# The first load of a low-rank update kernel as two transfers: 16 partitions, then 112

## The chip, the cores and the metric

The kernel runs on one core of a Trainium2 chip. The metric is device time in microseconds (us) for one execution, the median of the runs shown; lower is better. Engines are named as in the profile: PE (TensorE, matrix multiply), PEld (its weight loads), DVE (VectorE), ACT (ScalarE), POOL (GpSimd) and SP (SyncE, which here issues all DMA transfers; SPq is its queue). The core has 16 DMA engines, which all transfers share.

## What is computed

```python
def setup_inputs():
    batch, seq, d_model, r = 16, 512, 768, 16
    return {
        "x": np.random.randn(batch, seq, d_model).astype(np.float32),
        "A": np.random.randn(d_model, r).astype(np.float32) * 0.1,
        "B": np.random.randn(r, d_model).astype(np.float32) * 0.1,
        "scale": 0.5,
    }

def reference(x, A, B, scale):
    lora = np.matmul(np.matmul(x, A), B)
    return (x + scale * lora).astype(np.float32)
```

x is 8192 rows ("tokens") of 768 float32, 25.2 MB; the result is as large. A and B are 48 KB each.

## The kernel before

**Tiling.** The 8192 tokens lie in five parts of 8, 8, 16, 16 and 16 tokens per partition (`PARTS`). Within a part, partition p holds S consecutive tokens, so that n tokens of a partition are one contiguous run of n x 3072 bytes in memory (`memory`, L96 to L98). `x_all` in SBUF has room for 48 tokens a partition, the first four parts; the last part reuses the room of the first two. The work is done in 8 groups of 8 tokens per partition.

**Loads and stores.** `LOADS` (L106) cuts the parts into eight loads (part, first token, tokens): the first part is loaded as 2 tokens and then 6, the later ones as 8 or 16. Load k counts 16 on its own semaphore `s_load[k]` when it has landed. `STORES` (L129) has five stores. Everything goes through SP's one queue, in the order of `on_sync` (L136): load 0, load 1, a wait for POOL's memset of `a_rows` (`s_ready`), three transfers of A with 4 rows each, a wait for the memset of `b_rows`, the transfer of B with 16 rows (to every fourth partition of the first 64), loads 2 to 5, then stores 0 and 1 once the first two groups are summed, loads 6 and 7 as the room of the first part comes free, and the other stores. The last store stands behind the section, at L356 of the profile's kernel.

**Compute.** For each group: POOL and ACT cast x to float16 (`narrowed`, L188 to L199; it waits for the load that holds the tokens, once for each engine and load), DVE transposes in blocks of 32x32 (L255), PE multiplies with a block diagonal form of A (L285), ACT scales and spreads the product (L240), PE multiplies with B (L306), and DVE adds the result to x in place (L260). For group 0, POOL casts the first two tokens (from load 0), ACT the other six (from load 1). POOL also builds the operands from A and B at the start: `b_half` (L214) waits for B's rows, and DVE's transpose of A's rows (L248) for `s_a`, which counts the three transfers of A and POOL's first cast.

Of the kernel before, what the change touches and what calls it, by code (L numbers as in the profile page):

```python
# [28 lines left out]
def kernel(  # L29
# [10 lines left out]
    P = 128  # L40
# [3 lines left out]
    x2 = x.flatten_outer_dims()  # L44
# [38 lines left out]
    def sem(name):  # L83
        sems.append(nc.alloc_semaphore(name))
        return sems[-1]
# [10 lines left out]
    def memory(t2, i, s, n):  # L96
        S = PARTS[i]
        return t2[ds(parts[i], S * P), :].rearrange("(p s) d -> p s d", s=S)[:, ds(s, n), :]  # L98

    def held(i, s, n):  # L100
        return tiles(where.index((i, s)), n)

    def tiles(t, n):
        return x_all[:, ds(t % ROOM, n), :]

    LOADS = [  # L106
        (0, 0, 2), (0, 2, 6), (1, 0, 8), (2, 0, 8), (2, 8, 8), (3, 0, 16), (4, 0, 8), (4, 8, 8)
    ]
    s_load = [sem(f"s_load{k}") for k in range(len(LOADS))]

    def load_of(t):
        i, s = where[t]
        return next(k for k, ld in enumerate(LOADS) if ld[0] == i and ld[1] <= s < ld[1] + ld[2])
# [21 lines left out]

    def on_sync(e):  # L136
        def load(k):
            ld = LOADS[k]
            e.dma_start(out=held(*ld), in_=memory(x2, *ld)).then_inc(s_load[k], 16)  # L139

        def summed(k):
            e.wait_ge(s_sum, k + 1)
            if STORED[k] + 1 < NG:

                e.sem_inc(s_free[PAIRS - 1], 1)

        def store(k, done):
            st = STORES[k]
            e.dma_start(out=memory(out2, *st), in_=held(*st)).then_inc(done, 16)

        load(0)
        load(1)
        e.wait_ge(s_ready, 1)
        blocks = A.rearrange("(c e) r -> c (e r)", e=64)
        for c in range(SETS):
            e.dma_start(
                out=a_rows[c : SET * SET : SET, :], in_=blocks[ds(c * SET, SET), :]
            ).then_inc(s_a, 16)
        e.wait_ge(s_brows, 1)
        e.dma_start(out=b_rows[0 : R * APART : APART, :], in_=B).then_inc(s_b, 16)  # L160
        for k in range(2, len(LOADS) - 2):
            load(k)

        for p in range(2, PAIRS):
            e.sem_inc(s_free[p], 1)
        summed(0)
        summed(1)


        e.wait_ge(s_lora, 2 * PAIRS + 2)  # L170
        store(0, s_out0)
        store(1, s_out1)
        e.wait_ge(s_out0, 16)
        load(len(LOADS) - 2)
        e.wait_ge(s_out1, 16)
        load(len(LOADS) - 1)
        for k in range(2, len(STORES)):
            summed(k)
            if k == 2:


                e.wait_ge(s_raise, 6)
            if k + 1 < len(STORES):
                store(k, s_out)
# [3 lines left out]
    def narrowed(e, copy, g, first, n=SUB):  # L188
        t = g * GROUP + first
        for k in dict.fromkeys(load_of(t + k) for k in range(n)):  # L190
            if (e, k) not in here:
                here.add((e, k))
                e.wait_ge(s_load[k], 16)
        if g:
            e.wait_ge(s_taken, g)
        ins = copy(out=xn[:, ds(first, n), :], in_=tiles(t, n))  # L196

        ins.then_inc(s_narrow if g else s_first if first else s_a, 1)

    def on_gpsimd(e):  # L200
        e.memset(a_rows[0:Q], 0.0).then_inc(s_ready, 1)  # L201
        e.memset(b_rows, 0.0).then_inc(s_brows, 1)  # L202
        e.memset(pick, 0.0).then_inc(s_pick, 1)
        e.memset(w_bd.rearrange("p c k m -> p (c k m)").bitcast(fp32), 0.0)  # L204
        e.memset(y_bd.rearrange("p s m -> p (s m)").bitcast(fp32), 0.0).then_inc(s_ready, 1)  # L205
        e.wait_ge(s_pick, 1)
        e.affine_select(  # L207
            out=pick, in_=pick, compare_op=mybir.AluOpType.not_equal, fill=1.0, base=0,
            pattern=[[0, NQ], [-APART, Q]], channel_multiplier=1,
        ).then_inc(s_pick, 1)  # L210
        narrowed(e, e.tensor_copy, 0, 0, SUB // 2)
        e.wait_ge(s_pick, 2)
        e.wait_ge(s_b, 16)
        e.tensor_copy(out=b_half, in_=b_rows).then_inc(s_bh, 1)  # L214
        e.wait_ge(s_ready, 3)
        e.tensor_copy(  # L216
            out=w_one.rearrange("i (c e) k r -> i c e (k r)", c=SETS),
            in_=a_t[0:Q].rearrange("i k r (e c) -> i c e (k r)", c=SET)[:, 0:SETS, 0:SET, :],
        ).then_inc(s_w, 1)
        e.wait_ge(s_w, 1)  # L220
        for b in range(NQ):
            e.tensor_copy(  # L222
                out=w_bd[ds(b * Q, Q), :, :, ds(b * Q, R)], in_=w_one
            ).then_inc(s_w, 1)
            e.wait_ge(s_w, b + 2)
        for g in range(1, NG):
            narrowed(e, e.tensor_copy, g, SUB)

    def on_scalar(e):
        narrowed(e, e.copy, 0, SUB // 2, SUB // 2)  # L230
        narrowed(e, e.copy, 0, SUB)
        e.wait_ge(s_bp, 1)
        e.copy(out=b_mm, in_=lora[0][:, 0, :]).then_inc(s_bm, 1)  # L233
        for g in range(NG):
            if g + 1 < NG:
                narrowed(e, e.copy, g + 1, 0)
            e.wait_ge(s_y, g + 1)
            for b in range(NQ):
                q = ds(b * Q, Q)
                last = e.mul(out=y_bd[q, :, q], in_=y_ps[q, :, :], mul=sc)  # L240
                if b == 0 and g + 1 < NG:

                    last.then_inc(s_narrow, 1)
            last.then_inc(s_spread, 1)
# [151 lines left out]
```

## Time and profile before

| | us |
|---|---|
| median of 3 runs | 123.53 (123.52 to 123.67) |
| the profiled execution, its own time | 123.47 |
| its span, first to last instruction | 121.7 |
| granted TensorE clock, mean | 0.913 |

The span is the time between the first and the last profiled instruction of one execution; the rest of its time, 1.8 us, lies around it. The page gives for each engine its busy time and share, and cuts the span into 40 slices:

```profile
DMA  3999999999998997999999999997998899799790
GB/s 65 442 418 440 444 420 428 444 420 428 477 517 355 420 517 307 452 412 436 452 396 428 460 404 436 469 517 323 452 517 388 388 517 436 339 517 452 323 517 0
```

A digit is the mean busy share of the 16 DMA engines in that slice of 3 us, in tenths, and below it is what they moved in GB/s. Other views used are: the stretches (busy time by engine, DMA share and rate in chosen windows), the timeline of one engine, the waits (who waited for whom: total us, times, longest), the chain of waits (the chain that ended last, followed back from the last instruction) and the list of DMA issues with sizes and the time from issue to landing. In the timeline, "x2" is a merged run of two instructions, whose duration includes what lies between them. A DMA-issuing instruction ends when the transfer is handed on, long before its data has landed.

### The profile page before, as it was taken

To read this page: it belongs to the slowest core of one execution; us is meant where nothing else is said; L and a number is where in the kernel's file an instruction comes from. 1 tells how busy PE (TensorE), PEld (TensorE's weight loads), DVE (VectorE), ACT (ScalarE), POOL (GpSimd) and SP (SyncE) were. 2 spreads that over 40 slices of the span, in tenths; PEclk is the share of its full clock that TensorE was granted. 3 is DMA by queue.
4 is the path that set the end of the run, shared out by engine and by line. 5 is a ranking of instruction groups with operands and counts; after the bars stand their busy time and mean duration, and the time that the engine had idled before them with its cause. 6 is when DMAs were issued, how large, how long until landed. Compare 5 with 4: busy or idle time off the path is not lost.

```text
span 121.7 us, 889 instructions
## 1 busy us (share of the span) xinstructions
PE 50.7 (42%) x322; PEld 29.6 (24%) x322; DVE 81.7 (67%) x42; ACT 37.4 (31%) x43; POOL 28.4 (23%) x24
## 2 busy tenths in 40 slices
PE   0000239477457647745745744774674320000000
PEld 0000026243323424423423322442442110000000
DVE  0002850599999999999999989999995991000000
ACT  4003928526409313644440192733004000000000
POOL 7721638017009002604400170710000000000000
PEclk9999999999999999999999999999999995555555
DMA  3999999999998997999999999997998899799790
GB/s 65 442 418 440 444 420 428 444 420 428 477 517 355 420 517 307 452 412 436 452 396 428 460 404 436 469 517 323 452 517 388 388 517 436 339 517 452 323 517 0
DMA packets 1928, 50.43 MB, mean 414 GB/s; under 512 B 236, under 2 KB 236, under 8 KB 392
## 3 DMA queue, kind: packets, MB, share of 16 engines
q1 hardware_dynamic: 1928, 50.43, 97.0%
HBM read 25.26 MB, written 25.17 MB: 414 GB/s over the span
## 4 chain that ended last, share of the span: by engine, by line
DVE 34%; DMA 28%; PE 10%; ACT 9%; issue 1%; SPq 0%; POOLq 0%
DVE x_sb L260 22%; DMA x_sb<-in_x_dram 20%; DVE xt L255 12%; DMA out_dram<-x_sb 8%; PE ps_yt L285 6%; ACT xn L196 6%; PE lora_ps L306 3%; ACT y_bd L240 3%; SPq L139 0%; SPq L391 0%; POOLq L134 0%; POOLq L377 0%
## 5 line engine op out<-in xcount | busy, mean ns | idle before, releaser
L260 DVE TENSOR_TENSOR x_sb<-x_sb,lora_ps 128x1536 f32<-128x1536 f32 x32 | 53.7, 1734 | 1.4 <-PE lora_ps L306 1.4
L306 PE MATMUL lora_ps<-b_mm,y_bd 128*128 128x512 f16 (+1 forms) x128 | 25.0, 328 | 22.4 <-ACT y_bd L240 14.1
L196 ACT CAST xn<-x_sb 128x3072 f16<-128x3072 f32 (+1 forms) x9 | 23.4, 2609 | 35.4 <-DMA x_sb<-in_x_dram 25.7
L285 PE MATMUL ps_yt<-xt,w_bd 128*128 128x256 f16 x192 | 26.1, 288 | 12.7 <-DVE xt L255 12.7
L255 DVE STREAM_TRANSPOSE xt<-xn 128x3072 f32<-128x3072 f32 (+1 forms) x9 | 27.0, 3005 | 6.5 <-ACT y_bd L240 6.1
L196 POOL CAST xn<-x_sb 128x3072 f16<-128x3072 f32 (+1 forms) x8 | 20.7, 2586 | 44.7 <-DMA x_sb<-in_x_dram 26.2
L285 PEld LDWEIGHTS ps_yt<-xt,w_bd 128*128 128x128 f16 x192 | 18.9, 101 | 20.6 <-issue 15.8
L306 PEld LDWEIGHTS lora_ps<-b_mm,y_bd 128*128 128x128 f16 x128 | 10.6, 98 | 35.3 <-ACT y_bd L240 16.4
L240 ACT ACTIVATE y_bd<-ps_yt 32x256 f16<-32x256 f32 x32 | 12.0, 374 | 19.5 <-PE ps_yt L285 19.1
L248 DVE STREAM_TRANSPOSE a_t<-a_rows 32x1024 f32<-32x1024 f32 x1 | 1.9, 1943 | 11.3 <-DMA a_rows<-in_A_dram 11.3
L319 PE MATMUL lora_ps<-b_half,pick 128*128 128x512 f16 (+1 forms) x2 | 0.8, 500 | 12.5 <-POOL b_half L214 12.5
L319 PEld LDWEIGHTS lora_ps<-b_half,pick 128*128 128x128 f16 x2 | 0.1, 106 | 12.5 <-issue 12.5
L222 POOL COPY w_bd<-w_one 32x384 f16<-32x384 f16 x4 | 2.0, 499 | 0.2
L214 POOL CAST b_half<-b_rows 128x768 f16<-128x768 f32 x1 | 0.8, 827 | 4.6 <-DMA b_rows<-in_B_dram 4.6
L196 ACT ACT_TABLE_LOAD x1 | 1.3, 1283 | 0.9 <-PEq L377 0.9
L204 POOL MEMSET w_bd<- 128x1536 f32 x1 | 1.4, 1372 | 0.0
L201 POOL MEMSET a_rows<- 32x1024 f32 x1 | 0.9, 941 | 0.5 <-POOLq L134 0.5
L216 POOL CAST w_one<-a_t 32x384 f16<-32x384 f32 x1 | 0.8, 849 | 0.9 <-DVE a_t L248 0.9
L233 ACT CAST b_mm<-lora_ps 128x768 f16<-128x768 f32 x1 | 0.8, 798 | 0.0
L202 POOL MEMSET b_rows<- 128x768 f32 x1 | 0.7, 727 | 0.0
L205 POOL MEMSET y_bd<- 128x512 f32 x1 | 0.5, 514 | 0.0
L207 POOL TENSOR_SCALAR_AFFINE_SELECT pick<-pick 128x128 f16<-128x128 f16 x1 | 0.3, 298 | 0.0
(5 smaller groups left out, 0.6 us busy)
## 6 DMA issues: line engine op xcount, KB each, us to landing
out_dram<-x_sb SPq DMA_DIRECT2D x3, 6144.0 KB, 19.4
x_sb<-in_x_dram SPq DMA_DIRECT2D x5, 3072.0 KB, 14.6
x_sb<-in_x_dram SPq DMA_DIRECT2D x1, 6144.0 KB, 41.6
out_dram<-x_sb SPq DMA_DIRECT2D x2, 3072.0 KB, 13.8
x_sb<-in_x_dram SPq DMA_DIRECT2D x1, 2304.0 KB, 9.7
x_sb<-in_x_dram SPq DMA_DIRECT2D x1, 768.0 KB, 4.6
a_rows<-in_A_dram SPq DMA_DIRECT2D x3, 16.0 KB
b_rows<-in_B_dram SPq DMA_DIRECT2D x1, 48.0 KB, 7.5
```

Source lines behind the costliest of these rows:

```text
L196: ins = copy(out=xn[:, ds(first, n), :], in_=tiles(t, n))
L201: e.memset(a_rows[0:Q], 0.0).then_inc(s_ready, 1)
L204: e.memset(w_bd.rearrange("p c k m -> p (c k m)").bitcast(fp32), 0.0)
L214: e.tensor_copy(out=b_half, in_=b_rows).then_inc(s_bh, 1)
L222: e.tensor_copy(out=w_bd[ds(b * Q, Q), :, :, ds(b * Q, R)], in_=w_one).then_inc(s_w, 1)
L240: last = e.mul(out=y_bd[q, :, q], in_=y_ps[q, :, :], mul=sc)
L248: e.transpose(out=a_t[0:Q].rearrange("i k r c -> i (k r) c"), in_=a_rows[0:Q].rearrange("c (i k r) -> c (k r) i", k=2, r=R),).then_inc(s_r ...
L255: return e.transpose(out=ts[0], in_=ts[1])
L260: ins = e.tensor_tensor(out=xs, in0=xs, in1=lora[p % 2], op=mybir.AluOpType.add)
L285: mm = e.matmul(y_ps, w_bd[:, c, k, :], xv[:, :, c, :, k], start=(m == 0), stop=(m == MMS - 1),)
L306: mms.append(e.matmul(t[:, k, ds(n0, w)], y_bd[:, 2 * p + k, :], b_mm[:, ds(n0, w)], start=True, stop=True,))
L319: last = e.matmul(lora[0][:, 0, ds(n0, w)], pick.rearrange("p b r -> p (b r)"), b_half[:, ds(n0, w)], start=True, stop=True,)
```

## The change

Load 0, 2 tokens of each of 128 partitions (128 rows of 6144 bytes, 768 KB), is issued as two transfers on the same queue, one after the other: partitions 0 to 15, then partitions 16 to 127. Both count on `s_load[0]`, so whoever waits for load 0 waits for 32 counts and not 16 (`needs`). All other loads stay single transfers of 128 partitions, in the same order.

```diff
+    HEAD = 16
+    SHARES = {0: [(slice(0, HEAD), slice(0, 2)), (slice(HEAD, P), slice(0, 2))]}
+    needs = [16 * len(SHARES.get(k, [0])) for k in range(len(LOADS))]
...
         def load(k):
-            ld = LOADS[k]
-            e.dma_start(out=held(*ld), in_=memory(x2, *ld)).then_inc(s_load[k], 16)
+            i, s, n = LOADS[k]
+            for rows, cols in SHARES.get(k, [(slice(0, P), slice(s, s + n))]):
+                n = cols.stop - cols.start
+                e.dma_start(
+                    out=held(i, cols.start, n)[rows], in_=memory(x2, i, cols.start, n)[rows]
+                ).then_inc(s_load[k], 16)
...
             if (e, k) not in here:
                 here.add((e, k))
-                e.wait_ge(s_load[k], 16)
+                e.wait_ge(s_load[k], needs[k])
```

## The prediction

> **What bounds the kernel now.** I read the page's DMA lines first, because the page gives no compute engine more than 67% of the span.
>
> ```profile
> span 121.7 us, 889 instructions
> PE 50.7 (42%) x322; PEld 29.6 (24%) x322; DVE 81.7 (67%) x42; ACT 37.4 (31%) x43; POOL 28.4 (23%) x24
> q1 hardware_dynamic: 1928, 50.43, 97.0%
> DMA packets 1928, 50.43 MB, mean 414 GB/s; under 512 B 236, under 2 KB 236, under 8 KB 392
> ```
>
> One queue carries 50.43 MB, and its packets occupy 97.0% of the time of 16 DMA engines over the whole span. To see where the other 3% lie I cut the span into stretches (columns: stretch, length, busy time of five engines with instruction counts, granted clock, DMA share, GB/s).
>
> ```profile
> 0.00:0.90 0.90, 0.00 (x0) 0.00 (x0) 0.00 (x0) 0.01 (x1) 0.20 (x4) 1.00 0.00 0
> 0.90:1.90 1.00, 0.00 (x0) 0.00 (x0) 0.00 (x0) 1.00 (x1) 0.93 (x2) 1.00 0.00 0
> 1.90:2.90 1.00, 0.00 (x0) 0.00 (x0) 0.00 (x0) 0.27 (x1) 1.00 (x4) 1.00 1.00 147
> 2.90:4.40 1.50, 0.00 (x0) 0.00 (x0) 0.00 (x0) 0.00 (x0) 1.50 (x2) 1.00 0.97 385
> ...
> 5.10:9.90 4.80, 0.00 (x0) 0.00 (x0) 0.00 (x0) 0.00 (x0) 1.46 (x1) 1.00 1.01 434
> 9.90:11.10 1.20, 0.00 (x0) 0.00 (x0) 0.00 (x0) 0.02 (x1) 0.00 (x0) 1.00 1.12 466
> 11.10:44.70 33.60, 19.32 (x114) 11.24 (x114) 27.33 (x14) 17.65 (x18) 11.91 (x9) 1.00 1.00 432
> 44.70:55.00 10.30, 5.95 (x40) 3.55 (x40) 10.30 (x6) 4.25 (x5) 2.75 (x1) 1.00 1.00 432
> 55.00:74.40 19.40, 10.84 (x75) 6.68 (x76) 19.03 (x11) 8.50 (x10) 5.49 (x2) 1.00 1.01 433
> 74.40:101.50 27.10, 14.61 (x95) 8.13 (x93) 25.06 (x14) 5.75 (x9) 2.75 (x1) 0.98 1.00 433
> 101.50:119.40 17.90, 0.00 (x0) 0.00 (x0) 0.00 (x0) 0.00 (x0) 0.00 (x0) 0.50 0.99 428
> ```
>
> From 5.1 us to 119.4 us the queue never starves: 428 to 466 GB/s in every stretch, through all waits of the compute engines. So the time is the moment at which the stream reaches full rate, plus the bytes at about 433 GB/s, plus the tail. The change can act only on the start. There, nothing moves before 1.90, and the first microsecond carries 147 GB/s although the engines count as fully occupied: the first rows are in flight, but come slowly. Measured against 434 GB/s, the ramp has lost (434-147)x1.0/434 = 0.66 us by 2.90 and (434-385)x1.5/434 = 0.17 us more by 4.40: 0.83 us in all.
>
> Next the transfers of SyncE (SPq), which issues all of them, in order of time (start us, duration us). The first two were also looked at singly, and stand first.
>
> ```profile
> 0.89 0.38 SPq L139 DMA_DIRECT2D x_sb<-in_x_dram  x1
> 1.33 0.41 SPq L139 DMA_DIRECT2D x_sb<-in_x_dram  x1
> ```
>
> ```profile
> 1.94 2.00 SPq L156 DMA_DIRECT2D a_rows<-in_A_dram  x3
> 3.98 0.54 SPq L160 DMA_DIRECT2D b_rows<-in_B_dram  x1
> 4.57 2.04 SPq L139 DMA_DIRECT2D x_sb<-in_x_dram  x4
> 44.70 0.82 SPq L149 DMA_DIRECT2D out_dram<-x_sb  x2
> 55.01 7.84 SPq L139 DMA_DIRECT2D x_sb<-in_x_dram  x2
> ```
>
> The first load is issued at 0.89 and its first bytes move at 1.90, 1.01 us later. The second issue starts 0.44 us after the first (1.33-0.89).
>
> Last, what waits for the start, and how much margin it has:
>
> ```profile
> POOL b_half L214 <- DMA b_rows<-in_B_dram: 4.6, 1, 4.6
> POOL xn L196 <- DMA x_sb<-in_x_dram: 0.7, 1, 0.7
> ```
>
> ```profile
> 1.33 9.72 DMA x_sb<-in_x_dram
> 44.70 10.29 DMA out_dram<-x_sb
> ```
>
> ```profile
> x_sb<-in_x_dram SPq DMA_DIRECT2D x1, 6144.0 KB, 41.6
> x_sb<-in_x_dram SPq DMA_DIRECT2D x1, 2304.0 KB, 9.7
> x_sb<-in_x_dram SPq DMA_DIRECT2D x1, 768.0 KB, 4.6
> ```
>
> The 768 KB load lands 4.6 us after its issue, at about 5.5, and GpSimd's cast waits 0.7 us for it; after it GpSimd idles another 4.6 us for B's rows. The chain of waits does not even pass through the first load: it goes from SyncE's second issue through the 9.72 us of the second load. The 6144 KB load, last of the four issued from 4.57 on (issue near 6.2), lands near 6.2+41.6 = 47.8, while the first stores are issued at 44.70: compute is 3.1 us early for the queue.
>
> **The change, part by part.** All against the profiled execution: span 121.7 us, its own time 123.47 us, against 123.53 us, the median of the runs; I carry the difference to the median, so +0.06 goes to every time below.
>
> *Bytes.* The same 768 KB in 128 rows of 6 KB. The head is 16 rows, 96 KB (98,304 bytes); the rest is 112 rows, 672 KB. Sixteen engines have 1 and 7 rows each where they had 8. Sixteen more semaphore writes, one an engine, ride on the queue: 0 to 0.01 us, since the 236 packets under 512 bytes that the queue carries already, the semaphore writes among them, leave it at 433 GB/s.
>
> *SyncE.* One more issue, 0.38 to 0.41 us long and 0.44 us from start to start. The rest's issue starts at 1.33 instead of being part of the one at 0.89, the second load's at about 1.77 instead of 1.33, and it ends near 2.19. The transfers of A would start then and not at 1.94: +0.25 us for A, B and the four loads behind them, because SyncE stood from 1.74 to 1.94 for GpSimd's memset (0.97 to 1.91) anyway. Each is covered by the queue: the second load is needed only when the first is through, about 4.5 us; A and B pass when the second load is through, near 9.9; the loads issued at 4.57 are needed at 10.5. Covers of 2 to 5 us, against 0.25 to 0.44 us; without them each would cost its own delay on the stream. I take nothing for them.
>
> ```profile
> 0.97 0.94 POOL L201 MEMSET a_rows<- 32x1024 f32 x1 [0.53 <-POOLq L134]
> ```
>
> *The wait.* GpSimd's first cast now needs 32 semaphore counts. If the load lands some tenths later, so does the cast; behind it on GpSimd stands only the wait for B's rows with its 4.6 us, which hides it. ScalarE waits for the second load, which moves with the stream. The margin of 3.1 us at the first stores moves with the stream on both sides and stays. Nothing else is late next.
>
> *The start of the stream* is the only term. Seven rows an engine now come with an issue that starts 0.44 us later. In that time each engine has one row: 98,304 bytes at 434 GB/s is 0.23 us of work. With equal latency for both transfers the stream falls behind by 0.44-0.23 = **+0.21 us**. The trace shows no transfer cut this way, so I bound the term from both sides.
> - Below: if the rest finds the path warm, its bytes flow from 1.33+1.01 = 2.34 at full rate, 672 KB/434 GB/s = 1.59 us, and are through at 3.93. Now they are through at 4.54 (147+578 = 725 KB by 4.40, the other 62 KB at 434 GB/s in 0.14). That is -0.61 us, the floor.
> - Above: the head gives no cover at all (+0.44), and its rows are slow besides: 98 KB at the ramp's 147 GB/s take 0.67 us instead of 0.23, another 0.44. Together +0.88 us.
>
> The nearest row to a cut transfer in a filled queue is the stretch 9.9 to 11.1, where A's and B's transfers of 4 and 16 rows pass at 466 GB/s without loss; the nearest row to rows that start cold is 147 GB/s. The head starts cold, so I add a third of its 0.44, 0.15 us, to the 0.21: **+0.36 us**, from which 123.47+0.36+0.06 = 123.89 us.
>
> A page speaks against the change here. The Trainium skill, "SBUF — State Buffer", section "Door 1: The DMA port swizzle", says that the sixteen partitions 0 to 15 reach only 4 of 16 ports, some 109 GB/s. By it the head's 96 KB would take 0.90 us, the term would be about 0.21+0.67 = +0.88, and the time 124.4 (an estimate from that page). No run here shows it yet: B's sixteen rows, passing at 466 GB/s, go to partitions four apart.
>
> **The rivals.**
>
> *The head is spread badly (slower still).* The sixteen rows go to sixteen neighbouring partitions, and 112 rows are dealt out otherwise than 128; if engines get in one another's way, or the head isn't one row an engine at all, the whole of the upper price of slow rows counts: 0.21+0.44 = +0.65, 124.18 us. For it: 147 GB/s with all engines occupied shows that an occupied engine can move little. Against it: 466 GB/s with B's rows among the traffic.
>
> *It is hidden (same).* At 147 GB/s sixteen rows take 0.67 us, more than the 0.44 us until the rest arrives, so the queue may never run dry, and the rest meets engines still busy with the head: 0, 123.53 us. Against it: those eight rows are in flight together now, and reads asked for 0.44 us later can't come back as early.
>
> *The head warms the path (faster).* The slow part is the first row of an engine, not the number of rows; a head of sixteen starts all engines at once and pays the 0.66 us of the first microsecond while the rest is being issued. It gains as soon as the rest's own ramp costs less than the 0.61 us by which it could be early; with half of it paid, -0.30 us, 123.23 us. For it: the ramp is as large as 0.83 us, and of its first 1.0 us only a third is bytes. Against it: bytes can't move before 1.01 us after an issue, and the rest's issue is 0.44 us later. The Trainium skill ("Perfetto Trace Analysis", section "DMA Optimizations") says that splitting transfers can let some start sooner if the DMA engines are generally idle; here they are idle only before 1.90, which is where this rival would have to find its gain.
>
> **How the numbers follow.** The forecast, slower by arrival, has 0.42, with its own range 123.70 to 124.10; the bad spread 0.14; hidden 0.15; faster 0.29. No change means within 0.2%, 0.25 us, about what a measurement of this kernel can tell. Of the forecast 0.04 falls under that, of the faster case 0.02. Slower: 0.38+0.14 = 0.52; same: 0.15+0.04+0.02 = 0.21; faster: 0.27. The range runs from the faster case, 123.2, to the upper bound, 123.53+0.88 = 124.4.
>
> **What would show it.** SyncE: issues of the first load at 0.89 and near 1.33, the second load's near 1.77, A's near 2.2. Stream: the stretch 1.9 to 2.9 under 147 GB/s if the forecast holds, clearly over it in the faster case; the sum of bytes moved by 5 us decides between all four. From 5 us on every stretch again at 428 to 434 GB/s, only shifted, and the last landing, now 101.5+19.4 = 120.9, shifted by the same.
>
> ```profile
> L356 SPq DMA_DIRECT2D out_dram<-x_sb x1: 333/333/333, 101.5 to 101.5; - x1
> DMA to landing us min/median/max: 19.4/19.4/19.4
> ```
>
> I am wrong if the stream reaches 434 GB/s earlier than now, if the tail moves by another amount than the start, or if a stretch after 5 us loses rate.

## The result, and the profile after

The changed kernel takes 124.44 us (median of 4 runs, 124.38 to 124.85), the kernel before beside it 123.58 us (123.52 to 123.67). The ratio is 1.0076, 95% interval 1.0053 to 1.0099: slower by 0.94 us (0.65 to 1.22). The forecast was slower, 123.89 us, with a range up to 124.4; the direction held, and the loss is over twice the forecast one and just outside the range.

The stretches of the changed kernel, in the columns used before:

```profile
0.90:1.90 1.00, 0.00 (x0) 0.00 (x0) 0.00 (x0) 1.00 (x1) 0.93 (x2) 1.00 0.00 0
1.90:2.90 1.00, 0.00 (x0) 0.00 (x0) 0.00 (x0) 0.27 (x1) 1.00 (x4) 1.00 1.12 184
2.90:4.40 1.50, 0.00 (x0) 0.00 (x0) 0.00 (x0) 0.00 (x0) 1.50 (x2) 1.00 0.81 279
4.40:5.10 0.70, 0.00 (x0) 0.00 (x0) 0.00 (x0) 0.00 (x0) 0.42 (x2) 1.00 1.31 342
5.10:9.90 4.80, 0.00 (x0) 0.00 (x0) 0.00 (x0) 0.00 (x0) 1.47 (x1) 1.00 1.02 411
9.90:11.10 1.20, 0.00 (x0) 0.00 (x0) 0.00 (x0) 0.00 (x0) 0.00 (x0) 1.00 0.82 341
11.10:44.70 33.60, 18.47 (x111) 10.98 (x112) 26.57 (x14) 17.68 (x18) 11.92 (x9) 1.00 1.04 444
44.70:55.00 10.30, 6.33 (x45) 3.77 (x43) 10.30 (x6) 4.25 (x5) 2.75 (x1) 1.00 0.92 394
55.00:74.40 19.40, 10.78 (x75) 6.40 (x72) 18.18 (x10) 7.11 (x7) 5.50 (x2) 1.00 1.01 431
74.40:101.50 27.10, 15.02 (x96) 8.41 (x96) 25.43 (x14) 7.14 (x13) 2.75 (x1) 1.00 1.03 442
```

Nothing moves before 1.90, as before. The first stretch, with the head's sixteen rows and the first of the rest, has 184 GB/s instead of 147: a little quicker, not slower. Then the stream stays behind: 279 where it had 385, 342 where it had 456 (the row of the kernel before stands below), still 411 where it had 434, and 341 where it had 466. A row of data counts in the stretch in which it starts, so short stretches are rough: the 341 stands for rows that started just outside, and the 394 further down comes to 432, as before, together with the 444 ahead of it. If each row's bytes are counted evenly over its time in the trace, the changed stream is behind by 0.44 us at 5 us, 0.86 at 8, 0.86 at 11 and 0.99 at 20 (bytes short, at 434 GB/s).

```profile
4.40:5.10 0.70, 0.00 (x0) 0.00 (x0) 0.00 (x0) 0.00 (x0) 0.42 (x2) 1.00 1.16 456
```

The same in the list of issues (KB each, median us from issue to landing) and in the chain of waits (start us, us):

```profile
x_sb<-in_x_dram SPq DMA_DIRECT2D x1, 672.0 KB, 5.1
x_sb<-in_x_dram SPq DMA_DIRECT2D x1, 96.0 KB, 2.4
```

```profile
0.89 0.39 SPq L146
1.28 0.06 issue
1.35 0.40 SPq L146
1.75 0.04 issue
1.79 10.13 DMA x_sb<-in_x_dram
```

The rest is issued at 1.35 and lands 5.1 us later, at 6.45; the uncut load landed at 5.49. The second load is issued at 1.79 and lands at 11.92, before at 1.33+9.72 = 11.05. So 0.87 us are lost by the time the second load has landed, as much as the medians differ by (124.44-123.58 = 0.86). The profiled execution itself took 124.85 us, the most of the four and 1.38 more than the profiled one before; its other 0.5 us came later. By the even count the stream is 1.01 us behind at 70 us and 1.28 at 118. What happens after 70 us was not followed; the other three runs, 124.38 to 124.47, have no profile, but are too short for all of it.

### The profile page after: what moved, and what is told of

Same layout as the page of the kernel before. It is cut to its first block, busy times and chain, and to the rows that moved or that the text cites. A ratio compares the mean times of both kernels' runs of the same rounds, so it can differ in the third digit from the quotient of the medians.

```text
span 123.1 us, 890 instructions
## 1 busy us (share of the span) xinstructions
PE 50.6 (41%) x322; PEld 29.6 (24%) x322; DVE 81.7 (66%) x42; ACT 37.5 (30%) x43; POOL 28.4 (23%) x24
## 4 chain that ended last, share of the span: by engine, by line
DVE 34%; DMA 29%; PE 10%; ACT 9%; issue 1%; SPq 1%; POOLq 0%
DVE x_sb L269 22%; DMA x_sb<-in_x_dram 21%; DVE xt L264 12%; DMA out_dram<-x_sb 9%; PE ps_yt L294 6%; ACT xn L205 6%; PE lora_ps L315 3%; ACT y_bd L249 3%; SPq L146 1%; SPq L400 0%; POOLq L139 0%; POOLq L386 0%
## 6 DMA issues: line engine op xcount, KB each, us to landing
x_sb<-in_x_dram SPq DMA_DIRECT2D x1, 6144.0 KB, 42.4
```

## The experiments

Three theories. A, arrival: after the head the engines have too little to do until the second issue. B, span: a transfer into only some of the partitions makes engines write the same neighbourhood of SBUF, and the 112 rows pay for that. C: the sixteen rows of the head, all in one neighbourhood, are slow. A was the forecast's main term, C stood behind the 0.15 us added to it, and B was part of a rival. Losses below are (ratio-1) times the median of the kernel before in the same runs, with the interval's ends. The ratio is not that of the two medians; in the row of even and odd rows these differ by 1.77.

| kernel | us | before | ratio (95%) | loss, us |
|---|---|---|---|---|
| changed | 124.44 | 123.58 | 1.0076 (1.0053 to 1.0099) | 0.94 (0.65 to 1.22) |
| changed, again | 124.63 | 123.52 | 1.0095 (1.0074 to 1.0117) | 1.17 (0.91 to 1.45) |
| small columns first | 123.74 | 123.32 | 1.0043 (1.0030 to 1.0056) | 0.53 (0.37 to 0.69) |
| large columns first | 123.57 | 123.52 | 1.0013 (0.9999 to 1.0028) | 0.16 (-0.01 to 0.35) |
| 112 rows, then 16 | 124.61 | 123.32 | 1.0111 (1.0096 to 1.0126) | 1.37 (1.18 to 1.55) |
| head extra, 128 rows uncut | 123.96 | 123.32 | 1.0058 (1.0044 to 1.0071) | 0.72 (0.54 to 0.88) |
| 112 rows alone | 123.91 | 123.41 | 1.0041 (1.0026 to 1.0055) | 0.51 (0.32 to 0.68) |
| 64 rows, then 64 | 125.25 | 123.32 | 1.0155 (1.0141 to 1.0170) | 1.91 (1.74 to 2.10) |
| 64 and 64, read apart | 125.11 | 123.52 | 1.0141 (1.0125 to 1.0157) | 1.74 (1.54 to 1.94) |
| even rows, then odd | 125.29 | 123.52 | 1.0119 (1.0084 to 1.0153) | 1.47 (1.04 to 1.89) |
| two queues | 124.61 | 123.41 | 1.0082 (1.0055 to 1.0109) | 1.01 (0.68 to 1.35) |

**Columns in place of partitions, small piece first.**

```diff
+    CUTS = {0: [(0, 192), (192, 2 * D)]}
+    needs = [16 * len(CUTS.get(k, [0])) for k in range(len(LOADS))]
...
+            for c0, c1 in CUTS.get(k, []):
+                o, m = (v.rearrange("p s d -> p (s d)")[:, c0:c1] for v in (held(*ld), memory(x2, *ld)))
+                e.dma_start(out=o, in_=m).then_inc(s_load[k], 16)
```

> Load 0 is cut by columns and not by partitions: first 192 of the 1536 numbers of all 128 partitions (the same 96 KB, 768-byte rows), then the other 1344. Issues and bytes are those of the changed kernel, but every transfer has 128 partitions. Theory A (arrival: too little work is queued until the second issue) expects the changed kernel's loss here too, 0.2 us or more over the kernel before, up to the whole 0.86. Theory B (the 112 rows, dealt seven to an engine, make engines write the same partitions' neighbourhood) and theory C (the sixteen neighbouring rows of the head are slow) expect 0 to +0.2 us.

It lost 0.53 us, so a loss is there without any transfer that spans fewer than 128 partitions; but it is about half of the changed kernel's. Its stretches show where:

```profile
1.90:2.90 1.00, 0.00 (x0) 0.00 (x0) 0.00 (x0) 0.27 (x1) 1.00 (x4) 1.00 0.69 147
2.90:4.40 1.50, 0.00 (x0) 0.00 (x0) 0.00 (x0) 0.00 (x0) 1.50 (x2) 1.00 0.82 294
4.40:5.10 0.70, 0.00 (x0) 0.00 (x0) 0.00 (x0) 0.00 (x0) 0.42 (x2) 1.00 1.31 472
5.10:9.90 4.80, 0.00 (x0) 0.00 (x0) 0.00 (x0) 0.00 (x0) 1.46 (x1) 1.00 1.03 433
```

The loss is in 2.9 to 4.4: the DMA engines are occupied for 0.82 of the time, where the uncut load had 0.97, and move 294 GB/s for 385. From 4.4 on the rate is full. (The 0.69 in the first microsecond is no sign of the gap: the next kernel, without a gap, has 0.67 there.) The changed kernel is not yet at its full rate there (342 and 411), so something else goes on in it.

**The same cut, large piece first.**

```diff
-    CUTS = {0: [(0, 192), (192, 2 * D)]}
+    CUTS = {0: [(0, 1344), (1344, 2 * D)]}
```

> The cut by columns with the large piece (1344 of 1536 columns) first. Same two transfers as in the cut with the small piece first, other order. If the +0.42 us there came from arrival (A: too little is queued until the second issue), it is gone: 0 +-0.15 us. If a transfer more costs in itself, or rows of 768 bytes do, it stays: +0.3 to +0.5 us.

0.16 us, with an interval that touches 0. The same two sizes, in the order in which the queue does not run short, cost under a third of it, and in the stretch in which the other order lost, the rate is nearly that of the uncut load:

```profile
2.90:4.40 1.50, 0.00 (x0) 0.00 (x0) 0.00 (x0) 0.00 (x0) 1.50 (x2) 1.00 0.95 367
```

So a second transfer and rows of 768 bytes are not it, and the 0.53 us are mostly A.

**The 112 rows first, the 16 behind them.**

```diff
-    SHARES = {0: [(slice(0, HEAD), slice(0, 2)), (slice(HEAD, P), slice(0, 2))]}
+    SHARES = {0: [(slice(HEAD, P), slice(0, 2)), (slice(0, HEAD), slice(0, 2))]}
```

> The same two transfers, the 112 partitions first and the 16 behind them. Eight engines' rows are never short of work while the second issue is made, so A expects 0 (within 0.2 us of the kernel before). B expects +0.6 us or more, with long packets while the 112 rows move. C expects +0.4 us or more, with the loss only at the end of the load, when the sixteen rows move.

Here 112 rows are queued ahead of the second issue, the engines are occupied from 1.9 to 4.4 (0.94 and 1.03), and yet the loss is larger, 1.37 us. A alone falls with this run: with the first piece large enough, what is left is the span of the transfers, of the 112 rows or of the sixteen.

**The head as an extra, with load 0 uncut.**

```diff
+    spare = sb("spare", [16, 2, D], fp32)
...
+        e.dma_start(out=spare, in_=memory(x2, 0, 0, 2)[0:16]).then_inc(s_load[0], 16)
         load(0)
...
-                e.wait_ge(s_load[k], 16)
+                e.wait_ge(s_load[k], 32 if k == 0 else 16)
```

> The sixteen-row transfer goes first, into a spare buffer of 16 partitions, and load 0 follows uncut with its 128 partitions; 96 KB more are moved and nothing is computed from them. It has the head and no transfer of 112. The uncut load starts one issue later, so A expects +0.44 us (0.23 of extra bytes and the 0.21 of the gap). B expects no more than that, +0.2 to +0.44. C expects the head's own slowness on top, +0.8 us or more, with long packets in the head or right behind it.

0.72 us, of which 0.23 are the extra 96 KB; the other 0.49 (0.31 to 0.65) agree with the 0.53 (0.37 to 0.69) of the cut by columns, where the first piece lay over all partitions. So sixteen neighbouring rows at the cold start cost nothing that shows beside the gap behind them; intervals this wide leave room for a tenth or two. The trace of the changed kernel agrees: the head's rows take 360 ns each on average and are through at 2.46, when the first rows of the rest, from 2.38 on, have only begun. C falls for this place, as far as these runs can tell. Behind a full queue, as in the run above, they are not so cheap, or the 112 rows cost more without the gap; the two were not told apart.

**The 112 rows alone.** The sixteen rows of partitions 0 to 15 are not loaded but filled with zeros by GpSimd.

```diff
-    SHARES = {0: [(slice(0, HEAD), slice(0, 2)), (slice(HEAD, P), slice(0, 2))]}
+    SHARES = {0: [(slice(HEAD, P), slice(0, 2))]}
...
+        e.memset(x_all[0:HEAD, 0:2, :], 0.0).then_inc(s_zero, 1)
+        e.wait_ge(s_zero, 1)
```

> Load 0 is the one transfer into partitions 16 to 127; the sixteen rows of partitions 0 to 15 are left out (GpSimd fills them with zeros), so 96 KB fewer are moved, 0.23 us. No second issue and no head. If the 112 rows cost nothing in themselves and the changed kernel's loss is arrival and head alone, -0.23 us. If they cost what is left of the loss beside the 0.42 us of arrival, 0.45 to 0.7 us, then +0.2 to +0.5 us, with packets of 6144 bytes over 300 ns and slow first rows of load 1 after them.

It moves 0.23 us less and loses 0.51 us: the transfer into 112 partitions costs 0.74 us (0.55 to 0.91), with neither head nor second issue. The zeros hold nothing up on SyncE: A, B and the four loads are issued at 1.94, 3.98 and 4.57, as before. With the 0.53 of arrival the sum is 1.27, against 0.94 and 1.17 measured: the intervals overlap, and part of each may hide in the other. The stretches place the cost late:

```profile
4.40:5.10 0.70, 0.00 (x0) 0.00 (x0) 0.00 (x0) 0.00 (x0) 0.66 (x3) 1.00 1.35 404
5.10:9.90 4.80, 0.00 (x0) 0.00 (x0) 0.00 (x0) 0.00 (x0) 2.54 (x2) 1.00 0.99 422
9.90:11.10 1.20, 0.00 (x0) 0.00 (x0) 0.00 (x0) 0.00 (x0) 0.00 (x0) 1.00 1.11 417
```

These had 456, 434 and 466, and most of what moves in them is the second load and what follows it, not the 112 rows. The traces also hold the time of every single row. The second load is the same in all kernels, 128 rows of 18 KB, one to a partition; here is the mean time of the sixteen of its rows that start first, and of the others, each from one execution:

| load 0 | first sixteen rows of load 1, ns | other 112, ns |
|---|---|---|
| uncut (the kernel before) | 718 | 688 |
| small columns first | 715 | 691 |
| large columns first | 742 | 690 |
| head extra, 128 rows uncut | 711 | 688 |
| 112 rows alone | 976 | 691 |
| 16, then 112 (changed; again) | 1021; 1086 | 694; 705 |
| 112 rows, then 16 | 1326 | 694 |
| 64 rows, then 64 | 1130 | 694 |
| 64 and 64, read apart | 1126 | 690 |
| even rows, then odd | 945 | 754 |

Where the transfer just ahead of it went to all 128 partitions, the second load starts at 711 to 742 ns a row; where that went to fewer, at 945 to 1326. If each of the 16 engines has one of these rows, the 112 rows alone make the stream 0.26 us later here (976 for 718 ns; an estimate), and by another 0.11 at the first sixteen rows of 24 KB behind the second load (1029 for 917). The 112 rows themselves are through at 5.01, the uncut load's at 5.12 with 0.23 us more to move: 0.12 us late. Engines end at different times, so these need not add up to the 0.74, and the rest of it was not placed; but the larger parts fall on rows of the loads behind. In the changed kernel the last row of load 0 ends at 5.70, 0.58 later than before, and the second load's first rows add 0.30, which is about the 0.87 by which it lands late. Why a row is slow then, the trace doesn't say: its rows do not name the engine that moved them. That engines meet at the same part of SBUF, as B has it, stays argued.

**Two halves, 64 and 64.**

```diff
-    HEAD = 16
+    HEAD = 64
```

> Two transfers of 64 partitions each, four rows an engine. A expects 0: 384 KB are 0.9 us of work, twice the time between the issues. B and C (both say that what counts is which partitions a transfer spans) expect a larger loss than the changed kernel's: if 64 neighbouring partitions are written at half the rate, 768 KB take 3.6 us and not 1.8, so up to +1.8 us, and the second load's first rows are slow as well.

1.91 us, near the 1.8 that half rate would cost. The stretches show the rate itself:

```profile
1.90:2.90 1.00, 0.00 (x0) 0.00 (x0) 0.00 (x0) 0.28 (x1) 1.00 (x4) 1.00 0.54 98
2.90:4.40 1.50, 0.00 (x0) 0.00 (x0) 0.00 (x0) 0.00 (x0) 1.50 (x2) 1.00 0.98 270
4.40:5.10 0.70, 0.00 (x0) 0.00 (x0) 0.00 (x0) 0.00 (x0) 0.42 (x2) 1.00 1.05 237
5.10:9.90 4.80, 0.00 (x0) 0.00 (x0) 0.00 (x0) 0.00 (x0) 1.46 (x1) 1.00 1.03 374
9.90:11.10 1.20, 0.00 (x0) 0.00 (x0) 0.00 (x0) 0.00 (x0) 0.00 (x0) 1.00 1.04 445
```

From 2.9 to 5.1 the engines are occupied all the time (0.98 to 1.05) and move 237 to 270 GB/s, 0.55 to 0.62 of 434. The Trainium skill says in "SBUF — State Buffer", section "Door 1: The DMA port swizzle", that 64 neighbouring partitions reach half of the ports. By its figure, some 218 GB/s, the load would take 3.6 us instead of 1.8 (an estimate from that page); the run comes near it, at a somewhat higher rate. Part of the agreement in time is chance: the first rows of this kernel start at 2.26 and not at 1.91, behind an issue of 0.58 us instead of 0.38, so about 0.35 of the 1.91 us are a later start, and about 0.41 the second load's first rows (1130 ns for 718). That leaves some 1.15 for the rate itself (an estimate).

**Two halves of SBUF, read from all over memory.** The first transfer reads the even source rows and the second the odd ones, so tokens 0 and 1 of the first part get other rows' values.

```diff
                 e.dma_start(
-                    out=held(i, cols.start, n)[rows], in_=memory(x2, i, cols.start, n)[rows]
+                    out=held(i, cols.start, n)[rows],
+                    in_=memory(x2, i, cols.start, n)[slice(rows.start // HEAD, P, 2) if k == 0 else rows],
                 ).then_inc(s_load[k], 16)
```

> Two transfers into partitions 0 to 63 and 64 to 127 as in the run with HEAD = 64, but the first reads the even rows of the 128 source rows and the second the odd ones, so that each reads over the whole stretch of memory (tokens 0 and 1 of the first part get other rows' values). If the loss comes from where SBUF is written (B), it stays: +1.9 us (1.6 to 2.2). If it comes from what is read in memory, it goes down to that of a mere second issue, 0 to +0.5 us.

1.74 us (1.54 to 1.94): it stays. Where in memory the rows come from makes no difference that shows; which partitions they go to does.

**Even rows, then odd rows.**

```diff
-    SHARES = {0: [(slice(0, HEAD), slice(0, 2)), (slice(HEAD, P), slice(0, 2))]}
+    SHARES = {0: [(slice(0, P, 2), slice(0, 2)), (slice(1, P, 2), slice(0, 2))]}
```

> Two transfers of 64 rows again, even partitions first, odd ones second, source and destination alike. Each spans all partitions. If the count of rows below 128 is what slows a transfer (rows dealt out otherwise than for 128), the loss stays near +1.9 us. If it is that a transfer reaches only half of the partitions' neighbourhoods, it falls: 0 to +0.5 us. In between, if engines that are dealt neighbouring rows still meet in turns.

1.47 us, though both transfers reach over all partitions. But the loss is elsewhere:

```profile
2.90:4.40 1.50, 0.00 (x0) 0.00 (x0) 0.00 (x0) 0.00 (x0) 1.50 (x2) 1.00 0.90 336
4.40:5.10 0.70, 0.00 (x0) 0.00 (x0) 0.00 (x0) 0.00 (x0) 0.42 (x2) 1.00 1.41 518
5.10:9.90 4.80, 0.00 (x0) 0.00 (x0) 0.00 (x0) 0.00 (x0) 1.46 (x1) 1.00 0.97 361
9.90:11.10 1.20, 0.00 (x0) 0.00 (x0) 0.00 (x0) 0.00 (x0) 0.00 (x0) 1.00 0.80 343
```

Load 0 itself runs at a good rate (336 and 518, where the halves had 270 and 237); the second load, uncut and over all 128 partitions, then runs at 361. So reach over all partitions cures the transfer, as B says, but something is handed on to the next one: its first sixteen rows take 945 ns for 718, and here the other 112 are slow too, 754 for 688. With one first row and seven others an engine that makes 0.23+0.46 = 0.69 us (an estimate). Why, stays open. The first rows also start 0.36 us late, at 2.27, as with the two halves. The run's interval is the widest, and the profiled execution, 125.69, the slowest of its four (124.19 the fastest).

**The changed kernel again**, beside the cut with the large columns first and the two kernels of 64 rows above:

> The changed kernel once more, beside the next three on the same chip, so that sums of parts can be held against it: +0.86 us over the kernel before (0.65 to 1.1). If arrival and the span of partitions simply add, it is the cut by columns (+0.42) plus what the rest's 112 partitions cost.

1.17 us (0.91 to 1.45): the loss repeats, somewhat above the 0.65 to 1.1 expected, though not beyond its interval.

**Load 0 from ScalarE's queue, load 1 from SyncE's.** A side question: can the first microsecond be filled better?

```diff
-        load(0)
         load(1)
...
     def on_scalar(e):
+        e.dma_start(out=held(*LOADS[0]), in_=memory(x2, *LOADS[0])).then_inc(s_load[0], 16)
```

> The kernel before with load 0 issued from ScalarE's queue and load 1 from SyncE's at the same time. Every engine then has work on two queues from the start. If the slow first microsecond is a latency that every engine pays once, 0 +-0.15 us. If it is that too few rows are asked for at once, the first stretch carries more than 147 GB/s and the time falls by up to 0.4 us; slower by 0.2 us or more if the two queues get in each other's way.

Slower by 1.01 us (0.68 to 1.35). The load that the first cast needs now shares the engines with a load three times its size:

```profile
x_sb<-in_x_dram SPq DMA_DIRECT2D x1, 2304.0 KB, 10.2
x_sb<-in_x_dram ACTq DMA_DIRECT2D x1, 768.0 KB, 10.4
```

It lands after 10.4 us instead of 4.6. The first microsecond can be filled better, with 295 GB/s instead of 147, but the next stretch, to 4.4, falls to 311 from 385. The runs lie in two groups, 123.69 and 123.79 beside 124.56 to 124.82, and the profiled one is 123.79, so the profile doesn't show where the time went; this was not followed further. No kernel tried beats the one before.

## Why the prediction was right in direction and wrong in size

1. *DMA is the bound: right. Only the start of the stream moves: right in part.* The second load lands 0.87 us late, and three of the four runs end about as much later. But the stretch from 5.1 to 9.9 lost rate (411 for 434), which the forecast had named as a sign that it was wrong: by the even count 0.42 of the 0.86 us are lost between 5 and 8 us, when the second load's first rows move. The profiled run lost another 0.5 us later still. Compute is not late for the first stores: they are issued at 45.47, before the last of the loads ahead of them has landed, near 48.9 (its issue near 6.5, plus 42.4).
2. *Bytes, SyncE's issue, the wait for 32 counts: no cost that shows.* The issues came at 0.89, 1.35 and 1.79, A's at 2.26, as worked out (0.89, 1.33, 1.77, near 2.2). The large-first cut, which has the same extra issue, extra semaphore writes and doubled wait, costs 0.16 us (-0.01 to 0.35).
3. *Arrival, +0.21 us: right mechanism, too small.* It was 0.44 us between the issues minus 0.23 us of work in the head. Measured by columns it is 0.53 us (0.37 to 0.69), and by the extra head 0.49 (0.31 to 0.65). The work of the head brought nothing. One half of this the traces show: in the changed kernel the first sixteen rows of the rest start 0.48 us later than those of the uncut load (median 2.49 for 2.01) and take 844 ns each, no less than its 798, so the rest starts up as slowly as if it had been alone. The argument that eight rows in flight together hide one another's latency was given for the forecast, but was not priced: it would take away the 0.23 and leave the 0.44, which both measurements are near. That this is how the 0.23 are lost was not tried apart.
4. *"The head starts cold, so I add a third of its 0.44, 0.15 us": the step that failed.* It put the cost of the uneven spread on the sixteen rows, and nothing on the 112. The head cost nothing that shows (0.49 with it, 0.53 without), and its stretch was quicker than the cold start before (184 for 147 GB/s). The cost comes with the 112 rows: 0.74 us (0.55 to 0.91), five times the term, and most of what could be placed of it is paid by the rows of the loads behind them (976 ns for 718 in the 112 rows alone, 1021 in the changed kernel). The forecast had their dealing in half a sentence of a rival with 0.14 chance, and priced that rival, too, by the head's rows alone.
5. *The upper bound, +0.88.* It was built of arrival and head and had no term for the 672 KB of the rest. That the time lies so near the bound is luck: the measured parts, 0.53 and 0.74, are others than its 0.44 and 0.44. The 0.04 us by which it is passed are less than the runs scatter (124.38 to 124.85).
6. *The rule of the Trainium skill on ports* was weighed for the 16 partitions only. For 64 the rate came near it (237 to 270 GB/s for some 218). For the head at the cold start it was not seen: the estimate was 0.90 us, and the sixteen rows were through 0.55 us after the first of them started (1.91 to 2.46). Whether it has a part in what the 112 rows cost, no run shows.
7. *The lower bound, -0.61.* It took the uncut load to be through at 4.54. That counts rows where they start; the last one ended at 5.12.
8. *Hidden, and faster:* the changed stream never ran ahead after the first microsecond; the 37 GB/s more there were given back at once.

## What to carry to other kernels

Look at a split by partitions for all of its pieces, the large one above all: a transfer into 112 neighbouring partitions cost 0.74 us more than its bytes account for, and two of 64 cost 1.9, on a load of 1.8 us. Look also at the transfer behind it: much of the price was paid there. If a load must be cut, cut it by columns, so that each piece spans all partitions, and issue the large piece first: that cost nothing that could be measured surely. A small first transfer did not warm the queue up here (844 ns for the rest's first rows, 798 without a head); what mattered at the cold start was that the first issue brought enough to last until the second issue's rows flowed (0.16 us lost with the large piece first, 0.53 with the small one).

## What the runs showed of the hardware that was not expected

- A transfer that leaves out partitions slows the next one as well: after 112 rows the first rows of the following uncut load took 976 to 1086 ns for 718, and after even and odd rows that load ran at 361 GB/s from 5.1 to 9.9 for 434, though the cut load itself had kept up.
- The first microsecond of movement, 1.9 to 2.9, changes little with the cut: 147 GB/s uncut, 147 and 129 by columns, 154 to 197 with 16 or 112 rows. With 64 rows it is 98 to 104, because the first rows start 0.35 us later. Only two queues raised it much, to 295.
- Issues are not equal: those of the head and of the rest took 0.39 and 0.40 us, those of the two halves of 64 rows 0.58 and 0.57, as the chain of waits of that kernel shows:

```profile
0.89 0.58 SPq L146
1.47 0.06 issue
1.53 0.57 SPq L146
2.11 0.04 issue
2.15 10.55 DMA x_sb<-in_x_dram
```
